# One wide product for a weight's high part, and h's transposes side by side, in a two-layer attention trunk

## The chip, the cores and the metric

The kernel runs on one core of one Trainium2 chip. Its time is the device time of one execution in microseconds, as the median of several runs. Next to it stands one profiled execution, in which every instruction of every engine has a start and a length.

The engines go by the profile's names. PE is TensorE's matmuls and PEld its weight loads (the stationary operand); DVE is VectorE, ACT is ScalarE, POOL is GpSimd and SP is SyncE, which here only issues DMAs. Each engine works through its own queue in order. TensorE writes only to PSUM, of which there are eight banks of 128 partitions by 512 float32 values.

## The reference

Two layers over 256 tokens of width 1024, batch 1. All is float32. In a layer:

```python
x = x + 0.5 * swiglu(rms_norm(x, ffn1_norm[l]), ffn1_w_gate[l], ffn1_w_up[l], ffn1_w_down[l])
h = rms_norm(x, mix_norm[l])
proj = h @ w_in[l]                       # 1024 -> 2304
qa, ka, va, qb, kb, vb = jnp.split(proj, SPLITS, axis=-1)
out_a = windowed_gqa_sink(qa, ka, va, sink[l], slopes_a)          # 8 query heads, 2 key/value heads
out_b = differential_attention(qb, kb, vb, lam, slopes_b)         # 4 heads, two softmaxes each
out_b = (rms_norm(out_b, diff_subln[l]) * (1.0 - lam_init)).reshape(b, s, B_V_COLS)
x = x + jnp.concatenate([out_a, out_b], axis=-1) @ w_out[l]
x = x + 0.5 * swiglu(rms_norm(x, ffn2_norm[l]), ffn2_w_gate[l], ffn2_w_up[l], ffn2_w_down[l])
```

A final `rms_norm` ends it. `swiglu` is `(silu(h @ w_gate) * (h @ w_up)) @ w_down` with an inner width of 2816.

## The kernel before

**Numbers in two parts.** A float32 operand is split into a high part, the value rounded to `float32r`, and a low part, the rest. ScalarE rounds (`act.copy`) and VectorE subtracts (`dve.tensor_tensor`). A product is then three matmuls: high by high, high by low and low by high. All weights come by DMA into `raw` tiles and are split so, piece by piece, in `emit_split`.

**FFN.** Each layer has two. The inner width goes in groups of 512. The gate and up products of most groups are done "by sevens" (`by_sevens`): seven block products over sums and differences of the four blocks of x and of the gate and up weights take the place of eight. The sums of weights are made partly by DMAs of GpSimd's queue that add while they write (`gather` in `seven`), partly by VectorE (`plus`). `sevens=(2, 3, 4)` in the first FFN and `(1, 2, 3, 4)` in the other three, so there are 15 such groups. In the three FFNs that begin with group 1 the first group (`start` in the code) has no earlier group to work off. In a group by sevens the order on TensorE is: `p1`, the first block product; transposes of the earlier group's hidden block `h`, one token half at a time (`turn_one`); down products of earlier groups (`below`), 24 matmuls each; and the other six block products (`prod`), 12 matmuls each. ScalarE writes −p1 into both banks of the PSUM tile `xy`, and later products add onto it there. What is transposed is copied out of PSUM as high part (ScalarE) and low part (VectorE).

**Attention.** `mix` runs the combined input projection in groups of 256 output columns: two of keys for the differential heads (`first_groups`), two of queries for them, one of keys and values and two of queries for the windowed heads (`ngroup`); these seven call `narrow`. A weight chunk of 128 by 128 is the stationary operand and x, transposed, the moving one, its high part in columns 0 to 255 and its low part in 256 to 511 of `xv`. Per chunk there are three matmuls of 256 columns that all add into the same half of a bank. The result is multiplied by the tokens' reciprocal norms `R` on VectorE and split (`rmul` and `k_finish` for keys, `q_finish` for queries). Then come the scores, softmax with the bias of distance, transposes of the weights, the products with the values, the norm of the differential heads and the output projection.

**The order.** TensorE's instructions keep the program's order throughout; the other engines keep it in the FFNs, and in the attention they are ordered by the tile framework's planner. Weight pieces are split ahead of their use by a table, `LEAD`: at each `go()` or `weights()` the kernel calls `ahead(n)`, which emits DMAs and splits up to half-step n. So the table sets where in the queues of ScalarE and VectorE the splits stand. `seven` lists the loads of one group in the order in which they are used.

**PSUM.** `bank()` takes one of six banks; `pair()` takes the remaining two as one tile of 128 by 2 by 512.

All instructions are recorded by one helper, line 62, so the profile shows that line for every one of them, and the tile names tell them apart: `w` are split weights, `s` blocks of 128 by 2 by 512 (x, h and others), `q` and `v` the summed blocks of x and the queries, `raw` loaded weights.

Of the kernel before, what the change touches and what calls it, by code (L numbers as in the profile page):

```python
# [14 lines left out]
P = 128  # L15
D = 1024
S = 256
# [11 lines left out]
N_RAW, N_S4 = 6, 28  # L29
IN_FFN, IN_MIX = 8, 6  # L30
SEVEN = ((2, 3, 4), (1, 2, 3, 4))
LEAD = dict(start=(2, 8, 11, 9),
            open0=(2, 2, 0, 2, 2, 4, 8, 6, 7, 7, 8, 9, 4, 4, 7, 7, 7, 0),
            first=(1, 6, 6, 9, 12, 16, 16, 19, 19, 20, 22),
            mid=(6, 9, 9, 12, 15, 15, 17, 20, 20, 23, 24),
            last=(1, 8, 9, 12, 15, 15, 16, 18, 20, 21, 21),
            mid0=(1, 8, 12, 14, 15, 15, 20, 20, 20, 22, 22),
            last0=(4, 8, 11, 12, 15, 15, 17, 18, 20, 24, 24),
            first0=(2, 3, 5, 5, 5, 12, 12, 12, 12, 13, 13),
            open=(5, 10, 7, 14, 9, 11, 9, 3),  # L40
            close0=(3, 7, 10, 10, 6, 10, 5, 9, 6, 8, 2, 7, 2),
            close=(0, 8, 9, 9, 7, 10, 6, 7, 7, 7, 3, 7, 5),
            mix=(9, 3, 0, 2, 9, 2, 3, 5, 6, 8, 5, 4, 6, 1, 6, 7, 0, 4, 1, 9, 7, 8, 6, 11, 9, 9))


@with_exitstack
def trunk(ctx: ExitStack, tc: tile.TileContext, x, n1, g1, u1, d1, nm, w_in, sink,
# [31 lines left out]
    def nm_(s):  # L79
        uid[0] += 1  # L80
        return f"{s}_{uid[0]}"
# [2 lines left out]
        return ps.tile([P, 512], F32, tag="ps", bufs=6, name=nm_("ps"))  # L84

    def pair():
        return ps.tile([P, 2, 512], F32, tag="xy", bufs=1, name=nm_("xy"))

    def halves(b):
        return b.rearrange("p (a n) -> p a n", a=2)  # L90
# [40 lines left out]
    def seven(wg, wu, c0, below, down):  # L131

        a, b, c, d = [object() for _ in range(4)]
        w = {a: rows(wg, c0, 512, 0, 4), b: rows(wu, c0, 512, 0, 4), c: rows(wu, c0, 512, 4, 4), d: rows(wg, c0, 512, 4, 4)}

        def load(k):
            return lambda t: [(t, w[k])]  # L140

        def gather(k, to):
            def add():
                pool.dma_start(raws[to], w[k], accum_op=ALU.add)
            return add

        def plus(x, to):
            def prep():
                dve.tensor_tensor(raws[to], raws[to], raws[x], op=ALU.add)
            return prep  # L150

        steps = [Step(4, 512, load(b), key=b, behind=gather(c, b)), down, Step(4, 512, load(d), key=d, free=[])]
        if below is not None:
            steps.insert(0, below)
        else:
            steps.insert(0, steps.pop())
        steps[0].prep = lambda: issue(gather(b, a), 1)
# [477 lines left out]
    def narrow(acc, w, j, xs, kcs, first, last):  # L635

        for i, (wk, xk) in enumerate(kcs):
            wh, wl = w.part(wk, h=j)
            xv = xs[xk // 2][:, xk % 2]
            pe.matmul(acc, lhsT=wh, rhs=xv[:, 0:S], start=first and i == 0 and j == 0, stop=False)  # L640
            pe.matmul(acc, lhsT=wh, rhs=xv[:, S:512], start=False, stop=False)
            pe.matmul(acc, lhsT=wl, rhs=xv[:, 0:S], start=False, stop=last and i == len(kcs) - 1 and j == 1)

    def first_groups(norm, ws):

        both = pair()
        sls = [halves(both[:, i]) for i in range(2)]
        for k in range(0, KC, 2):
            norm.late(k // 2)
            for w, sl in zip(ws, sls):  # L650
                for j in range(2):
                    narrow(sl[:, j], w, j, norm.xs, KALL[k:k + 2], k == 0, k == KC - 2)
        norm.spread(bank())
        return sls

    def ngroup(norm, w):
        sl = halves(bank())
        for j in range(2):
            narrow(sl[:, j], w, j, norm.xs, KALL, True, True)
        return sl  # L660

    class Residual:
# [24 lines left out]
    def ffn(norm, aside=None, before=None, final=False, sevens=SEVEN[1]):  # L687
# [31 lines left out]
                pe.matmul(acc, lhsT=xh, rhs=lo, start=False, stop=k == 3, skip_group_check=not first)  # L719
            return acc  # L720

        def turn_one(h, t):
            sl = bank()
            for k in range(4):
                pe.transpose(sl[:, k * P:(k + 1) * P], h[:, t, k * P:(k + 1) * P], ident)
            hb = blk()
            act.copy(hb[:, 0], sl)
            dve.tensor_tensor(hb[:, 1], sl, f(hb[:, 0]), op=ALU.subtract)
            return hb
# [14 lines left out]
        def by_sevens(h, groups, old):  # L744
# [5 lines left out]
            for g in groups:  # L750
                start, late = old is None, g == groups[-1]
                first = 2 * at["use"] - (2 if start else 0)
                caps = iter(LEAD[("first" if start else "last" if late else "mid") + "0" * (stage == 0)])

                def go():
                    ahead(first + next(caps))

                go()
                p1 = prod(norm.quarter(0, 0), take())
                act.activation(xy, p1.unsqueeze(1).to_broadcast([P, 2, 512]), AF.Copy, scale=-1.0)  # L760
                new = [turn_one(h, 0)]
                go()
                if start:
                    new.append(turn_one(h, 1))
                    go()
                    prod(norm.quarter(0, 1), take(), p1)
                else:
                    below(old, g - 2, 1, take())
                    new.append(turn_one(h, 1))
                    go()  # L770
                prod(norm.summed(0), take(), xy[:, 0])
                go()
                below(by_token(new), g - 1, 0, take())
                go()
                if not start:
                    prod(norm.quarter(0, 1), take(), p1)
                g0 = silu(flat(), p1, 0)
                go()
                old = by_token(new)
                p5 = prod(norm.summed(1), take())  # L780
                act.copy(p1, p5)
                go()
                prod(norm.summed(2), take(), xy[:, 1])
                go()
                prod(norm.summed(3), take(), p5)
                e = flat()
                act.copy(e, p5)
                u1, u0 = flat(), flat()
                dve.tensor_tensor(u0, xy[:, 1], e, op=ALU.add)
                dve.tensor_tensor(u1, xy[:, 0], e, op=ALU.add)  # L790
# [37 lines left out]
        def both():  # L828
            p = pair()
            return [p[:, t] for t in range(2)]  # L830

        gs, us = [bank(), bank()], both()
        if before is None:
            before = norm.late
        look[0] = IN_FFN
# [42 lines left out]
        for n in range(1, NGRP):  # L878
# [10 lines left out]
            tokens(gs, norm.xs, weights(), 4)  # L889
            g = gate(gs)  # L890
            next(sums, None)
            us = both()
            for k0 in (0, 4):
                tokens(us, norm.xs, weights(), k0)
                next(sums, None)
# [3 lines left out]
                if hh == 0:  # L899
                    next(sums, None)  # L900

        gu = both()
        tokens(gu, norm.xs, weights(), 0)
        hT = turn(h, 2)
        tokens(gu, norm.xs, weights(), 4)
# [53 lines left out]
    def mix(l, norm, nxt_norm):  # L959
# [7 lines left out]
            for i in range(n):  # L967
                kbs[names[i]] = kt[:, i]

        def rmul(sl):  # L970
            t = tmp()
            dve.tensor_tensor(t, sl, bc(norm.R), op=ALU.mult)
            return t

        def q_finish(sl, sc):
            t = tmp()
            q = tp.tile([P, 2, 512], F32R, tag="q", bufs=3, name=nm_("q"))
            with urgent():
                for i in range(2):
                    dve.scalar_tensor_tensor(t[:, i], in0=sl[:, i], scalar=sc[i], in1=norm.R, op0=ALU.mult, op1=ALU.mult)  # L980
                split(q, t)
            return [q[:, 0], q[:, 1]]

        def scores(q, kb, dist, slopes, init, den, wide=False):

            both = pair() if wide else None
            sl = [both[:, i] if wide else bank() for i in range(2)]
# [43 lines left out]

        s0, s1 = first_groups(norm, (weights(held=True), weights(2, True)))
        kept[0] = False
        k_finish(rmul(s0), 2, [("b", 0), ("b", 1)])
        k_finish(rmul(s1), 2, [("b", 2), ("b", 3)])
        q0 = q_finish(ngroup(norm, weights()), [qscB[:, 0:1], qscB[:, 1:2]])
        q1 = q_finish(ngroup(norm, weights()), [qscB[:, 2:3], qscB[:, 3:4]])
        tkv = rmul(ngroup(norm, weights()))
        a_b = [soft_b(0, q0[0]), soft_b(1, q0[1])]
        k_finish(tkv, 1, ["a"])  # L1040

# [29 lines left out]
        vsl = [both[:, t] for t in range(2)]  # L1071
        for k0 in (0, 4):
            w = weights()
            for k in range(4):
# [41 lines left out]

        oT = [blk() for _ in range(4)]
        rsl, both = [bank() for _ in range(2)], pair()
        osl = [both[:, t] for t in range(2)]
        for t in range(2):  # L1120
            for h in range(HB):
                for kc in range(2):
# [173 lines left out]
```

## Time and profile before

| | |
|---|---|
| median of 3 runs | 916.47 us (916.43 to 916.83) |
| the profiled execution | 916.47 us, of which the span is 914.7 us |
| TensorE busy | 906.1 us, 4710 matmuls |
| VectorE busy | 767.5 us |
| ScalarE busy | 600.1 us |
| DMA | 200.87 MB, mean 220 GB/s |

The page lists the busy time of each engine, then the chain of work that ended last, then groups of instructions: their count, their busy time, the mean length of one, and the idle time before them with what ended it. Matmuls are pipelined, so the mean length of a matmul (389 ns for 512 columns) is more than the distance from one start to the next; counting the distance needs the starts. In a timeline a row is the start in us, the time from the first start to the last end, the engine, and what it did, with the count.

### The profile page before, as it was taken

How to read it: one execution, taken by the hardware profiler on the slowest of the kernel's cores; microseconds unless marked ns; L12 is line 12 of the kernel's file. 1: busy time of each engine (PE TensorE's matmuls, PEld its weight loads, DVE VectorE, ACT ScalarE, POOL GpSimd, SP SyncE). 2: the span in 40 equal slices, each digit the busy share in tenths (PEclk: the TensorE clock that was granted, in tenths of full speed). 3: DMA queues.
4: the chain of work that ended last, by engine and by line, in shares of the span. 5: the costliest groups of instructions: out<-in, count | busy, mean ns of one | idle time of the engine just before them, and what ended most of it. 6: DMA issues, size and time to landing. Idle time of an engine off the chain costs nothing.

```text
span 914.7 us, 12449 instructions
## 1 busy us (share of the span) xinstructions
PE 906.1 (99%) x4710; PEld 766.4 (84%) x4710; DVE 767.5 (84%) x1033; ACT 600.1 (66%) x932; POOL 66.9 (7%) x83
## 2 busy tenths in 40 slices
PE   9999999999999999999999999999999999999997
PEld 8888888899888888888888888888998888888886
DVE  5959999778876899999688999996786878999984
ACT  6936778465875776677485676675576685776660
POOL 0501000000000101000010101000001010101011
PEclk9999999999999999999999999999999999999999
DMA  9998897953436798897858898897722758898821
GB/s 333 346 275 222 243 296 246 264 140 134 140 137 186 183 286 240 235 298 257 278 140 236 240 295 259 231 310 196 206 71 90 247 115 237 232 305 249 241 100 47
DMA packets 114061, 200.87 MB, mean 220 GB/s; under 512 B 3662, under 2 KB 31376, under 8 KB 114000
## 3 DMA queue, kind: packets, MB, share of 16 engines
q1 hardware_dynamic: 97344, 167.53, 54.0%
q0 software_dynamic: 16096, 31.75, 20.1%
q8 instruction: 37, 0.61, 0.3%
q10 hardware_dynamic: 560, 0.79, 0.2%
q14 instruction: 24, 0.20, 0.1%
HBM read 199.00 MB, written 1.05 MB: 219 GB/s over the span
## 4 chain that ended last, share of the span: by engine, by line
PE 98%; issue 0%; ACT 0%; DVE 0%; POOL 0%; POOLq 0%
PE ps L62 73%; PE xy L62 26%; ACT xy L62 0%; DVE s L62 0%; DVE xk L62 0%; POOLq L1291 0%; POOL rf L62 0%; POOL ident masks.py:199 0%; POOL ident masks.py:197 0%; DVE tot L62 0%; POOLq masks.py:199 0%; DVE tmp L62 0%; POOLq L1282 0%
## 5 line engine op out<-in xcount | busy, mean ns | idle before, releaser
L62 DVE TENSOR_TENSOR w<-raw,w 128x1024 fp32r<-128x1024 f32 (+1 forms) x458 | 478.9, 1098 | 39.5 <-ACT w L62 38.6
L62 PE MATMUL ps<-w,s 128*128 128x512 f32 (+1 forms) x2046 | 478.1, 390 | 0.7 <-ACT xy L62 0.7
L62 ACT CAST w<-raw 128x1024 fp32r<-128x1024 f32 (+1 forms) x458 | 404.5, 952 | 74.3 <-DVE raw L62 58.9
L62 PEld LDWEIGHTS ps<-w,s 128*128 128x128 f32 x2046 | 379.4, 188 | 78.9 <-ACT xy L62 1.4
L62 PE MATMUL xy<-w,s 128*128 128x512 f32 x528 | 125.8, 392 | 0.0
L62 PEld LDWEIGHTS xy<-w,s 128*128 128x128 f32 x528 | 98.3, 188 | 20.4
L62 PE MATMUL xy<-w,q 128*128 128x512 f32 x360 | 87.8, 393 | 0.0
L62 PEld LDWEIGHTS xy<-w,q 128*128 128x128 f32 x360 | 66.7, 188 | 13.4
L62 POOL DMA_DIRECT2D raw<-in_ffn_w_up_dram x30 | 38.9, 1314 | 422.5 <-DVE w L62 285.3
L62 DVE TENSOR_TENSOR raw<-raw,raw 128x2048 f32<-128x2048 f32 x30 | 68.6, 2288 | 0.5
L62 PE MATMUL ps<-s,w 128*128 128x256 f32 x480 | 59.2, 284 | 0.0
L62 PEld LDWEIGHTS ps<-s,w 128*128 128x128 f32 x480 | 58.1, 192 | 0.4
L62 ACT ACTIVATE s<-ps,gcol 128x256 fp32r<-128x256 f32 (+1 forms) x80 | 31.8, 478 | 40.2 <-PE ps L62 40.2
L62 ACT CAST s<-ps 128x512 fp32r<-128x512 f32 x44 | 24.9, 587 | 32.6 <-PE ps L62 32.6
L62 DVE TENSOR_TENSOR s<-ps,s 128x512 fp32r<-128x512 f32 x44 | 29.4, 684 | 18.7 <-ACT s L62 18.7
L62 PE MATMUL ps<-w,q 128*128 128x512 f32 x180 | 43.2, 389 | 0.0
L62 PE MATMUL ps<-w,v 128*128 128x512 f32 x180 | 43.2, 389 | 0.0
L62 PE MATMUL ps<-ident,s 128*128 128x128 f32 x304 | 41.2, 273 | 0.0
L62 PEld LDWEIGHTS ps<-ident,s 128*128 128x128 f32 x304 | 35.7, 141 | 6.1 <-issue 0.8
L62 PEld LDWEIGHTS ps<-w,q 128*128 128x128 f32 x180 | 33.8, 188 | 7.0
L62 PEld LDWEIGHTS ps<-w,v 128*128 128x128 f32 x180 | 33.8, 188 | 7.0
L62 ACT ACTIVATE s<-s,negm 128x256 f32<-128x256 f32 x64 | 31.8, 499 | 11.1 <-DVE negm L62 9.9
(120 smaller groups left out, 529.5 us busy)
## 6 DMA issues: line engine op xcount, KB each, us to landing
raw<-in_ffn_w_down_dram SPq DMA_DIRECT2D x44, 1024.0 KB, 6.6
raw<-in_ffn_w_gate_dram SPq DMA_DIRECT2D x39, 1024.0 KB, 6.8
raw<-in_ffn_w_up_dram SPq DMA_DIRECT2D x39, 1024.0 KB, 6.7
raw<-in_ffn_w_up_dram POOLq DMA_DIRECT2D x30, 1024.0 KB, 9.4
raw<-in_w_in_dram SPq DMA_DIRECT2D x14, 1024.0 KB, 5.6
raw<-in_ffn_w_gate_dram SPq DMA_DIRECT2D x8, 512.0 KB, 7.0
raw<-in_ffn_w_up_dram SPq DMA_DIRECT2D x8, 512.0 KB, 8.5
raw<-in_w_in_dram SPq DMA_DIRECT2D x8, 512.0 KB, 7.6
```

The source lines that it names most:

```text
L62: ins = issue(*a, **k)
```

## The change

Five things change.

1. In `narrow` the high part of a weight chunk is multiplied by both parts of x in one product of 512 columns, into a whole bank; the low part is multiplied by x's high part, 256 columns, and added to the bank's second half. A group of 256 output columns so fills two banks. The new `whole` adds the two halves of each bank: ScalarE copies the second half to SBUF, with the scale, VectorE adds the first half, and VectorE multiplies by `R`. `rmul` goes, and `q_finish` calls `whole`.
2. `pair()` becomes a list of two tiles of one bank each. Where ScalarE wrote −p1 to both banks by one instruction, two now write one bank each.
3. In a group by sevens that isn't the first, the transposes of both token halves stand together, after the down product; those of the second half go to `xy[1]`, which gets its −p1 later, after the product onto `xy[0]`. The transposes are issued as matmuls with `is_transpose`, with the start flag on the first of four and the stop flag on the last.
4. In a first group by sevens the product onto `xy[0]` is moved before the product that adds onto p1; in `seven` the two loads swap places.
5. Every row of the look-ahead table `LEAD` is rewritten.

```diff
 LEAD = dict(...
-            first=(1, 6, 6, 9, 12, 16, 16, 19, 19, 20, 22),
-            mid=(6, 9, 9, 12, 15, 15, 17, 20, 20, 23, 24),
+            first=(1, 1, 1, 7, 12, 15, 16, 19, 19, 22, 22),
+            mid=(2, 8, 12, 12, 15, 15, 20, 20, 20, 22, 23),
...
     def pair():
-        return ps.tile([P, 2, 512], F32, tag="xy", bufs=1, name=nm_("xy"))
+        return [ps.tile([P, 512], F32, tag="xy", bufs=2, name=nm_("xy")) for _ in range(2)]
...
         else:
-            steps.insert(0, steps.pop())
+            steps.insert(1, steps.pop())
...
             xv = xs[xk // 2][:, xk % 2]
-            pe.matmul(acc, lhsT=wh, rhs=xv[:, 0:S], start=first and i == 0 and j == 0, stop=False)
-            pe.matmul(acc, lhsT=wh, rhs=xv[:, S:512], start=False, stop=False)
-            pe.matmul(acc, lhsT=wl, rhs=xv[:, 0:S], start=False, stop=last and i == len(kcs) - 1 and j == 1)
+            pe.matmul(acc, lhsT=wh, rhs=xv, start=first and i == 0, stop=False)
+            pe.matmul(acc[:, S:512], lhsT=wl, rhs=xv[:, 0:S], start=False, stop=last and i == len(kcs) - 1)
...
-        both = pair()
-        sls = [halves(both[:, i]) for i in range(2)]
+        sls = [[bank(), bank()], pair()]
...
-                    narrow(sl[:, j], w, j, norm.xs, KALL[k:k + 2], k == 0, k == KC - 2)
+                    narrow(sl[j], w, j, norm.xs, KALL[k:k + 2], k == 0, k == KC - 2)
...
     def ngroup(norm, w):
-        sl = halves(bank())
+        sl = [bank(), bank()]
...
-        def turn_one(h, t):
-            sl = bank()
+        def turn_one(h, t, sl=None):
+            sl = bank() if sl is None else sl
             for k in range(4):
-                pe.transpose(sl[:, k * P:(k + 1) * P], h[:, t, k * P:(k + 1) * P], ident)
+                pe.matmul(sl[:, k * P:(k + 1) * P], lhsT=h[:, t, k * P:(k + 1) * P], rhs=ident,
+                          is_transpose=True, start=k == 0, stop=k == 3)
...
                 p1 = prod(norm.quarter(0, 0), take())
-                act.activation(xy, p1.unsqueeze(1).to_broadcast([P, 2, 512]), AF.Copy, scale=-1.0)
-                new = [turn_one(h, 0)]
+                act.activation(xy[0], p1, AF.Copy, scale=-1.0)
+                if start:
+                    act.activation(xy[1], p1, AF.Copy, scale=-1.0)
+                    new = [turn_one(h, 0)]
+                    go()
+                    new.append(turn_one(h, 1))
+                    go()
+                else:
+                    below(old, g - 2, 1, take())
+                    go()
+                    new = [turn_one(h, 0), turn_one(h, 1, xy[1])]
+                    go()
+                prod(norm.summed(0), take(), xy[0])
+                if not start:
+                    act.activation(xy[1], p1, AF.Copy, scale=-1.0)
                 go()
                 if start:
-                    new.append(turn_one(h, 1))
-                    go()
                     prod(norm.quarter(0, 1), take(), p1)
-                else:
-                    below(old, g - 2, 1, take())
-                    new.append(turn_one(h, 1))
-                    go()
-                prod(norm.summed(0), take(), xy[:, 0])
-                go()
                 below(by_token(new), g - 1, 0, take())
...
-        def rmul(sl):
+        def whole(sl, sc=(1.0, 1.0)):
+
             t = tmp()
-            dve.tensor_tensor(t, sl, bc(norm.R), op=ALU.mult)
+            for i, b in enumerate(sl):
+                act.activation(t[:, i], b[:, S:512], AF.Copy, scale=sc[i])
+            for i, b in enumerate(sl):
+                dve.scalar_tensor_tensor(t[:, i], in0=b[:, 0:S], scalar=sc[i], in1=t[:, i], op0=ALU.mult, op1=ALU.add)
+            dve.tensor_tensor(t, t, bc(norm.R), op=ALU.mult)
             return t

         def q_finish(sl, sc):
-            t = tmp()
             q = tp.tile([P, 2, 512], F32R, tag="q", bufs=3, name=nm_("q"))
             with urgent():
-                for i in range(2):
-                    dve.scalar_tensor_tensor(t[:, i], in0=sl[:, i], scalar=sc[i], in1=norm.R, op0=ALU.mult, op1=ALU.mult)
-                split(q, t)
+                split(q, whole(sl, sc))
             return [q[:, 0], q[:, 1]]
```

The remaining edits replace `xy[:, i]` and `both[:, t]` by the new pair's items.

More of the change, by code (lines that the diff above doesn't have):

```diff
@@ L31 @@
 SEVEN = ((2, 3, 4), (1, 2, 3, 4))
-LEAD = dict(start=(2, 8, 11, 9),
-            open0=(2, 2, 0, 2, 2, 4, 8, 6, 7, 7, 8, 9, 4, 4, 7, 7, 7, 0),
-            first=(1, 6, 6, 9, 12, 16, 16, 19, 19, 20, 22),
-            mid=(6, 9, 9, 12, 15, 15, 17, 20, 20, 23, 24),
[L36 to L43, printed above, removed]
+LEAD = dict(start=(5, 7, 10, 10),
+            open0=(2, 0, 0, 2, 6, 6, 8, 6, 5, 6, 1, 10, 2, 5, 7, 7, 8, 0),
+            first=(1, 1, 1, 7, 12, 15, 16, 19, 19, 22, 22),
+            mid=(2, 8, 12, 12, 15, 15, 20, 20, 20, 22, 23),
+            last=(1, 7, 12, 14, 15, 15, 17, 20, 20, 21, 22),
+            mid0=(6, 9, 12, 14, 15, 15, 19, 19, 19, 22, 24),
+            last0=(2, 8, 12, 13, 15, 15, 19, 20, 20, 23, 25),
+            first0=(2, 3, 3, 4, 7, 11, 11, 14, 14, 18, 18),
+            open=(8, 12, 11, 9, 11, 11, 9, 5),
+            close0=(7, 5, 7, 5, 6, 10, 3, 10, 5, 11, 4, 7, 1),
+            close=(1, 8, 9, 9, 6, 8, 8, 9, 1, 7, 5, 4, 6),
+            mix=(10, 2, 0, 2, 9, 2, 3, 5, 6, 11, 5, 2, 3, 1, 6, 5, 2, 4, 1, 6, 7, 8, 6, 11, 7, 8))
 @with_exitstack
@@ L656, in ngroup @@
     def ngroup(norm, w):
-        sl = halves(bank())
+        sl = [bank(), bank()]
         for j in range(2):
-            narrow(sl[:, j], w, j, norm.xs, KALL, True, True)
+            narrow(sl[j], w, j, norm.xs, KALL, True, True)
         return sl
@@ L782, in by_sevens @@
                 go()
-                prod(norm.summed(2), take(), xy[:, 1])
+                prod(norm.summed(2), take(), xy[1])
                 go()
@@ L788, in by_sevens @@
                 u1, u0 = flat(), flat()
-                dve.tensor_tensor(u0, xy[:, 1], e, op=ALU.add)
-                dve.tensor_tensor(u1, xy[:, 0], e, op=ALU.add)
+                dve.tensor_tensor(u0, xy[1], e, op=ALU.add)
+                dve.tensor_tensor(u1, xy[0], e, op=ALU.add)
                 h = blk(F32)
@@ L825, in down @@
             tokens(accs[h], [None] * (2 * g) + hT, w, 4 * g, last=(FC - 1, G4 - 1) if final and h else FC - 1)
[L828 to L832, printed above, removed]
+        gs, us = [bank(), bank()], pair()
         if before is None:
@@ L891, in ffn @@
             next(sums, None)
-            us = both()
+            us = pair()
             for k0 in (0, 4):
@@ L900, in ffn @@
                     next(sums, None)
-        gu = both()
+        gu = pair()
         tokens(gu, norm.xs, weights(), 0)
@@ L986, in scores @@
             both = pair() if wide else None
-            sl = [both[:, i] if wide else bank() for i in range(2)]
+            sl = [both[i] if wide else bank() for i in range(2)]
             for t in range(2):
@@ L1033, in mix @@
         kept[0] = False
-        k_finish(rmul(s0), 2, [("b", 0), ("b", 1)])
-        k_finish(rmul(s1), 2, [("b", 2), ("b", 3)])
+        k_finish(whole(s0), 2, [("b", 0), ("b", 1)])
+        k_finish(whole(s1), 2, [("b", 2), ("b", 3)])
         q0 = q_finish(ngroup(norm, weights()), [qscB[:, 0:1], qscB[:, 1:2]])
         q1 = q_finish(ngroup(norm, weights()), [qscB[:, 2:3], qscB[:, 3:4]])
-        tkv = rmul(ngroup(norm, weights()))
+        tkv = whole(ngroup(norm, weights()))
         a_b = [soft_b(0, q0[0]), soft_b(1, q0[1])]
@@ L1070, in mix @@
         both = pair()
-        vsl = [both[:, t] for t in range(2)]
+        vsl = both
         for k0 in (0, 4):
@@ L1118, in mix @@
         rsl, both = [bank() for _ in range(2)], pair()
-        osl = [both[:, t] for t in range(2)]
+        osl = both
         for t in range(2):
```

## The prediction

> **What bounds the kernel now.** I read the first part of the page, then the chain of work that ended last, then the waits.
>
> ```profile
> span 914.7 us, 12449 instructions
> PE 906.1 (99%) x4710; PEld 766.4 (84%) x4710; DVE 767.5 (84%) x1033; ACT 600.1 (66%) x932; POOL 66.9 (7%) x83
> PE 98%; issue 0%; ACT 0%; DVE 0%; POOL 0%; POOLq 0%
> ...
> PEld ps L62 <- ACT xy L62: 1.4, 3, 0.5
> ```
>
> TensorE works through the whole span and is 98% of the chain, so time leaves only as TensorE instructions, or as the small waits between them. VectorE has 16% of the span free and ScalarE 34%: room on average, not everywhere. The last row is a wait that the change touches: three times about 0.5 us before a weight load, on ScalarE's copy into `xy`.
>
> A busy TensorE may still run slowly, so the next thing is the spacing of matmuls, read off long unbroken pieces of the chain (start, length, count):
>
> ```profile
> 100.53 10.88 PE ps L62 x48
> ...
> 189.47 8.63 PE xy L62 x72
> ```
>
> 48 products of 512 columns take 10.88 us, 226.7 ns each; 72 of 256 columns take 8.63 us, 119.9 ns each. The difference, 106.8 ns for 256 columns, is 0.417 ns a column; what is left, 13.1 ns, comes with each instruction whatever its width.
>
> **Wide products.** The narrow ones are these two groups:
>
> ```profile
> L62 PE MATMUL ps<-s,w 128*128 128x256 f32 x480 | 59.2, 284 | 0.0
> L62 PE MATMUL xy<-s,w 128*128 128x256 f32 x192 | 23.8, 284 | 0.0
> ```
>
> 480 + 192 = 672 products are 224 triples (2 layers, 7 groups, 8 chunks, 2 halves). A triple becomes one product of 512 columns and one of 256: 3 × 119.9 = 359.7 ns against 226.7 + 119.9 = 346.6 ns. The columns stay, one instruction goes: 13.1 × 224 = 2.93 us, all on the path. A weight load goes with it; a load is hidden today behind every 119.9 ns product, so it is hidden behind a wider one.
>
> The Trainium skill, "TensorE: Matmul & The Clock Gate", section "Back-to-back issue gap", gives a warm matmul N/2.4 + 2.5 ns. By it the fixed part would be 2.5 ns, and the removed instructions an estimated 0.56 us; our rows disagree with its constant (13.1 ns), agree with its slope, and decide. By the page the sum below would be 914.3 us.
>
> **Transposes together.** In the groups by seven the two tokens' transposes stand apart today, with 24 products between; elsewhere eight stand together:
>
> ```profile
> 181.94 1.03 PE L62 MATMUL ps<-ident,xk 128*128 128x128 f32 x8
> 182.73 3.00 PE L62 MATMUL ps<-w,s 128*128 128x512 f32 x12
> 185.56 3.03 PE L62 MATMUL xy<-s,w 128*128 128x256 f32 x24
> ...
> 334.16 0.60 PE L62 MATMUL ps<-ident,s 128*128 128x128 f32 x4
> 334.51 5.74 PE L62 MATMUL ps<-w,s 128*128 128x512 f32 x24
> 340.09 0.60 PE L62 MATMUL ps<-ident,s 128*128 128x128 f32 x4
> 340.45 2.99 PE L62 MATMUL xy<-w,q 128*128 128x512 f32 x12
> 343.27 3.11 PE L62 MATMUL ps<-w,s 128*128 128x512 f32 x13
> ```
>
> From start to start, four cost 5.93 − 24 × 0.2267 = 0.49 us, and the next four 3.18 − 2.72 = 0.46: 0.95 together. Eight in one run cost 3.62 − 2.72 = 0.90. Leaving and entering transposes once less is worth 0.05 us. Of the 15 groups by seven three are first groups, where the eight already stand together, so 12 × 0.05 = 0.6 us. I cost the start and stop flags at nothing: the instruction and its shape stay.
>
> The price is that both halves of `h` are now finished in the 12 products before the down products, where one was. Today:
>
> ```profile
> 369.92 3.48 DVE L62 TENSOR_TENSOR w<-raw,w 128x1024 fp32r<-128x1024 f32 x3
> 373.33 0.68 DVE L62 TENSOR_TENSOR s<-ps,s 128x512 fp32r<-128x512 f32 x1
> ...
> 374.14 4.24 PE L62 MATMUL ps<-w,s 128*128 128x512 f32 x18
> ```
>
> The second half's subtraction ends at 374.01; the low part of that token is first wanted by the fifth product, 374.14 + 4 × 0.227 = 375.05. That is 1.0 us in hand; a further 128x512 subtraction in VectorE's queue takes 0.6 to 0.7. It fits with 0.3 to spare, if no more weight pieces (3.48/3 = 1.16 us each) stand ahead of it. I take nothing here, and price the other case as a rival. The second token's transposes go to `xy[1]`, so ScalarE's later write of −p1 there waits for that subtraction; behind it queue ScalarE's weight copies. ScalarE has a third of its time free, and p1 itself is first added to after another 24 products (5.4 us), so I take nothing there either.
>
> **The first groups.** Here the waits named above lie:
>
> ```profile
> 308.28 1.03 PE L62 MATMUL ps<-ident,s 128*128 128x128 f32 x8
> 309.54 3.02 PE L62 MATMUL ps<-w,s 128*128 128x512 f32 x12 [0.23 <-ACT xy L62]
> 312.39 2.88 PE L62 MATMUL xy<-w,q 128*128 128x512 f32 x12
> ...
> 308.48 1.01 ACT L62 ACTIVATE xy<-ps 128x1024 f32<-128x1024 f32 x1 [3.35 <-PE ps L62]
> ...
> L62 ACT COPY ps<-ps 128x512 f32<-128x512 f32 x15 | 8.6, 572 | 25.0 <-PE ps L62 25.0
> ```
>
> 4.11 − 2.72 = 1.39 us for eight transposes, 0.49 more than without a wait: the next product adds onto p1, which ScalarE reads until 309.49 to write both banks of `xy`. Reordered, the product onto `xy[0]` comes next. A PSUM copy of one bank takes 0.57 us, so `xy[0]` stands at 308.48 + 0.57 = 309.05; with the 0.05 us between ScalarE's end and TensorE's start now, TensorE resumes at 309.10, not 309.54. I take 0.44 × 3 = 1.3 us (at best 1.5; at worst 0, if the wait only changes its name). The second copy, 0.57 us, ends long before p1 is added to, 12 products later; it delays the two halves' copies on ScalarE by no more than today's double copy does. Late next are the weights of the step that is moved forward by 2.7 us, whose second part GpSimd's queue adds by DMA. That transfer is early:
>
> ```profile
> 276.34 1.34 POOL L62 DMA_DIRECT2D raw<-in_ffn_w_up_dram  x1 [17.91 <-DVE w L62]
> 297.91 1.32 POOL L62 DMA_DIRECT2D raw<-in_ffn_w_up_dram  x1
> raw<-in_ffn_w_up_dram POOLq DMA_DIRECT2D x30, 1024.0 KB, 9.4
> ```
>
> Issued at 276.34 and landing some 9.4 us later, it is over 20 us ahead of 309. SyncE's loads of the two steps swap places; no DMA is added.
>
> **Halves added by VectorE.** Each group of projections now has two ScalarE copies of 256 columns from PSUM, two VectorE operations and one multiplication, before the split.
>
> ```profile
> 182.00:260.00 78.00, 78.00 (x637) 71.99 (x636) 60.08 (x168) 50.04 (x137) 3.53 (x4) 1.00 0.42 122
> L62 ACT ACTIVATE s<-ps,gcol 128x256 fp32r<-128x256 f32 (+1 forms) x80 | 31.8, 478 | 40.2 <-PE ps L62 40.2
> L62 DVE SCALAR_TENSOR_TENSOR tmp<-ps,qscB,R 128x256 f32<-128x256 f32 x8 | 3.5, 476 | 0.0
> L62 DVE TENSOR_TENSOR tmp<-ps,R 128x512 f32<-128x512 f32 x2 | 1.4, 692 | 4.4 <-PE ps L62 4.4
> ...
> 215.84 0.69 DVE L62 TENSOR_TENSOR tmp<-ps,R 128x512 f32<-128x512 f32 x1 [2.20 <-PE ps L62]
> 239.48 0.48 DVE L62 CUSTOM_DVE_ANT_0 s<-ps,distA,nsnk 128x256 f32<-128x256 f32 x1
> 242.20 1.09 PE L62 MATMUL ps<-ident,s 128*128 128x128 f32 x8
> ```
>
> A layer's ScalarE gets 14 × 0.48 = 6.7 us more; VectorE 3 × (2 × 0.48) = 2.9 for key and value groups, whose multiplication stays (0.69), and 4 × 0.69 = 2.8 for the q groups, whose scaling moves into the additions: 5.7 us. In this layer the first row has VectorE busy for 60.08 of 78 us and ScalarE for 50.04: 18 and 28 us free. The early groups meet idle VectorE (2.20 us before 215.84 alone). The late ones do not: the last key-value group and both windowed q groups put 0.96 + 2 × 0.69 = 2.3 us into the softmax stretch. The nearest work behind it are the transposes at 242.20, whose banks come free when the second head pair's bias step ends, about 239.9: 2.3 us in hand, and TensorE comes 32 × 0.013 = 0.4 us earlier. So the need, 2.7, exceeds the margin by 0.4, less what VectorE's idle time in between and its movable weight pieces give back. Bounds: nothing, and 2.7 us a layer; I take 0.15, nearer nothing, 0.3 us in all. In PSUM a group holds two of six banks instead of one, free again some 2 us after its end while the group two later comes 5.5 us on: nothing.
>
> **The look-ahead table** is rewritten throughout. It adds and removes no work, only places weight pieces. Bounds: it can remove only the waits that remain, under 1 us; one piece put badly costs up to 1.2 us wherever a margin is short. I take zero, the first row having shown almost no wait to mend.
>
> **Sum.** −2.93 − 0.6 − 1.3 + 0.3 = −4.5 us. The profiled execution took 916.47 us around its 914.7 span, and the median of the runs is also 916.47: 912.0 us.
>
> **Rivals.** (1) Slower: the halves of `h` come late. If the new table leaves one more weight piece (1.16 us) ahead of the two subtractions, the 0.3 us to spare becomes a wait of 0.85 us in each of 12 groups, 10 us: 922 us. It decides from 0.5 us a group on (4.5 + 1.8 us over 12 reaches 918.3). For it: the queue above already holds three pieces in front. Against: today's order keeps 1.0 us in hand in every group, and VectorE's load there does not grow. 11%.
> (2) The projections' additions push the softmax: 0.7 to 2 us of wait a layer instead of 0.15, that is 913.1 to 915.7, about 914.3. For it: 2.7 against 2.3 above. Against: weight pieces fill that queue and can move. 14%.
> (3) The wide product saves nothing, the 13.1 ns being of switching operands and not of issue: 914.9 us. Against: both widths show the same remainder. By the skill's constant, 914.3, close to this case. 5%.
>
> **How the numbers follow.** The forecast, 910.9 to 913.4 (full waits gained and nothing lost; half the first groups' gain and 0.4 us more lost a layer), has 70%. A measurement tells 0.2%, 1.8 us, from no change: faster is below 914.6, slower above 918.3. Faster: 70 + 8 of (2) + 1 of (3) = 79%; slower: 10 of (1); same: the remaining 11%. The range, 910.6 to 916.0, adds (2) and (3) to the forecast and leaves out (1) and little else.
>
> **What would show it.** Products of 512 and 256 columns alternating at 346.6 ns a pair; 4486 matmuls, if all are recorded; TensorE's three waits on `xy` near 0.05 us; eight transposes at 0.90 us in 15 places; VectorE near 779 and ScalarE near 615 us. Wrong would be waits of the down products on VectorE's `s`, of scores or transposes on VectorE in the softmax stretch, or of any product on `w`.

## The result and the profile after

The changed kernel takes 911.84 us (median; 911.71 to 912.20) against 916.50 us, a ratio of 0.9949 with a 95% interval of 0.9932 to 0.9966: 4.66 us less. Timed again beside other kernels, it took 912.22 us against 916.50. The forecast was 912.0 us. Its profiled execution took 912.20 us, of which the span is 910.4 us.

The page and the weight loads' waits, in the order in which the prediction read them:

```profile
span 910.4 us, 12060 instructions
PE 902.3 (99%) x4486; PEld 754.2 (83%) x4486; DVE 777.5 (85%) x1053; ACT 613.8 (67%) x975; POOL 64.9 (7%) x83
...
PEld ps L62 <- issue: 3.3, 13, 0.4
PEld ps L62 <- POOL ident masks.py:199: 1.4, 1, 1.4
PEld ps L62 <- ACT tmp L62: 0.8, 2, 0.4
PEld ps L62 <- DVE s L62: 0.7, 1, 0.7
```

TensorE is still busy for the whole span, with 224 matmuls fewer. VectorE has 10.0 us more to do and ScalarE 13.7 us more, and the span is shorter all the same. The wait on ScalarE's `xy` is gone from the list. The largest new wait that names an engine came once: a weight load waited 0.7 us for VectorE's `s`. The row `issue` is time for which the profile names no cause.

The projections, where three groups follow one another and where one stands between scores. First the windows of the kernel before, then the same pieces after the change (first the stretch and its length, then each engine's busy time and count):

```profile
198.19:215.73 17.54, 17.54 (x146) 17.38 (x145) 13.88 (x24) 10.02 (x19) 0.00 (x0) 1.00 0.64 201
217.35:223.29 5.94, 5.94 (x50) 5.81 (x49) 5.02 (x23) 4.22 (x17) 0.00 (x0) 1.00 0.00 1
```

```profile
197.92:214.84 16.92, 16.92 (x98) 14.72 (x96) 16.57 (x30) 13.78 (x28) 0.00 (x0) 1.00 0.65 218
216.47:222.31 5.84, 5.84 (x34) 4.89 (x32) 5.77 (x26) 4.83 (x19) 0.00 (x0) 1.00 0.49 174
```

Three groups, 48 triples, became 0.62 us shorter, 12.9 ns a triple. The group between scores became only 0.10 us shorter, 6 ns for each of its 16 triples. Over an attention the start of the stage's transposes shows what is left at its end: 230.95 before, 229.87 after, and 185.56 and 185.66 for the first projection, so 1.18 us a layer, 2.3 to 2.4 in both.

The first group by seven that has no earlier group, after the change:

```profile
307.19 1.03 PE L62 MATMUL ps<-ident,s 128*128 128x128 f32 x8
308.02 3.01 PE L62 MATMUL xy<-w,q 128*128 128x512 f32 x12
310.87 1.30 PE L62 MATMUL ps<-w,s 128*128 128x512 f32 x5
...
307.39 1.07 ACT L62 ACTIVATE xy<-ps 128x512 f32<-128x512 f32 x2 [2.19 <-PE ps L62]
```

From the transposes to the end of the 12 products is 3.68 us, 0.96 without the products' 2.72, where it was 1.39. And a group that isn't the first, its transposes now eight in a row:

```profile
338.08 0.60 PE L62 MATMUL ps<-ident,s 128*128 128x128 f32 x4
338.51 0.60 PE L62 MATMUL xy<-ident,s 128*128 128x128 f32 x4
338.87 2.98 PE L62 MATMUL xy<-w,q 128*128 128x512 f32 x12
341.68 1.52 PE L62 MATMUL ps<-w,s 128*128 128x512 f32 x6
```

3.60 − 2.72 = 0.88 us, where two times four cost 0.95.

So the traces agree with each term to within 0.6 us: 2.3 to 2.4 us in the projections, 3 × 0.43 = 1.3 in the first groups, 12 × 0.05 to 0.07 in the others. What they can't show is what part of it the rewritten table carries.

### The profile page after: what moved, and what is told of

Same layout as the page of the kernel before. It is cut to its first block, busy times and chain, and to the rows that moved or that the text cites. A ratio compares the mean times of both kernels' runs of the same rounds, so it can differ in the third digit from the quotient of the medians.

```text
span 910.4 us, 12060 instructions
## 1 busy us (share of the span) xinstructions
PE 902.3 (99%) x4486; PEld 754.2 (83%) x4486; DVE 777.5 (85%) x1053; ACT 613.8 (67%) x975; POOL 64.9 (7%) x83
## 4 chain that ended last, share of the span: by engine, by line
PE 91%; DMA 5%; DVE 1%; ACT 1%; issue 1%; POOL 0%; SPq 0%; POOLq 0%; ACTq 0%
PE ps L62 69%; PE xy L62 22%; DMA raw<-in_ffn_w_up_dram 4%; DVE w L62 1%; DMA raw<-in_ffn_w_gate_dram 1%; ACT w L62 1%; ACT junk L62 0%; POOL r L62 0%; ACT s L62 0%; DVE s L62 0%; ACT tmp L62 0%; SPq L172 0%; DVE xk L62 0%; DVE q L62 0%; POOLq L1293 0%
## 5 line engine op out<-in xcount | busy, mean ns | idle before, releaser
L62 PE MATMUL ps<-s,w 128*128 128x512 f32 (+1 forms) x384 | 70.2, 339 | 0.0
L62 ACT CAST s<-ps 128x512 fp32r<-128x512 f32 x32 | 18.1, 593 | 36.5 <-PE ps L62 36.3
L62 DVE TENSOR_TENSOR s<-ps,s 128x512 fp32r<-128x512 f32 x32 | 21.3, 688 | 18.0 <-ACT s L62 17.9
L62 PE MATMUL ps<-ident,s 128*128 128x128 f32 x256 | 34.0, 273 | 0.0
L62 PEld LDWEIGHTS ps<-ident,s 128*128 128x128 f32 x256 | 29.7, 140 | 4.8 <-issue 0.8
```

The lines of the kernel that those rows point to most:

```text
L62: ins = issue(*a, **k)
```

## The experiments

The theory to test is the prediction's: the three edits save TensorE's time each by itself, and the table is worth nothing. The rivals are that the gain is the table's, or that the edits fit only together with it. Each kernel was timed in turn with the kernel before on the same chip; its ratio to that is given with its 95% interval.

**The wide product, issued as two.** From the changed kernel:

```diff
-            pe.matmul(acc, lhsT=wh, rhs=xv, start=first and i == 0, stop=False)
+            pe.matmul(acc[:, 0:S], lhsT=wh, rhs=xv[:, 0:S], start=first and i == 0, stop=False)
+            pe.matmul(acc[:, S:512], lhsT=wh, rhs=xv[:, S:512], start=False, stop=False)
```

> The changed kernel, with each wide product of 512 columns issued as two of 256; all else stays, the additions on VectorE and ScalarE too. Theory (each matmul instruction has a fixed part of 13.1 ns, on the path): 224 more instructions, 2.4 to 2.9 us slower than the changed kernel, 914.2 to 914.8 us. Rival (the gain came from the new table and the order, not from the instructions): no slower, 911.8 us.

914.25 us, 0.9978 (0.9969 to 0.9986) of before: 2.0 to 2.4 us more than the two medians of the changed kernel. Here the columns, the banks, the additions and the table are as in the changed kernel, so the 224 added products cost this. Each brings a weight load of its own (4710 of both again), and no run parts a product's price from its load's. The timeline has the three groups back at their old length:

```profile
197.55 17.61 PE L62 MATMUL ps<-s,w 128*128 128x256 f32 x144
215.09 0.98 PE L62 MATMUL ps<-s,q 64*128 64x256 f32 x12
```

215.09 − 197.55 = 17.54 us.

**The wide products alone.** The kernel before, with `narrow`, `whole`, the pair of two tiles and the two banks a group, and nothing else.

```diff
+            pe.matmul(acc, lhsT=wh, rhs=xv, start=first and i == 0, stop=False)
+            pe.matmul(acc[:, S:512], lhsT=wl, rhs=xv[:, 0:S], start=False, stop=last and i == len(kcs) - 1)
...
-        k_finish(rmul(s0), 2, [("b", 0), ("b", 1)])
+        k_finish(whole(s0), 2, [("b", 0), ("b", 1)])
```

> The kernel before with the wide products and the additions of halves alone; order, transposes and look-ahead table as before. Theory (the parts add up, and the table is worth nothing): 2.4 us faster than before, the amount by which the attention stages of the two traces differ, 914.1 us. Rival (the additions fit only with the new table): waits in the softmax stretch eat the gain, 915.5 us or more.

914.16 us, 0.9976 (0.9967 to 0.9985): 2.23 us less, with the interval some 1.4 to 3.0. The new work of VectorE and ScalarE costs no time that shows, with the old table too.

**The first groups alone.**

```diff
-            steps.insert(0, steps.pop())
+            steps.insert(1, steps.pop())
...
-                act.activation(xy, p1.unsqueeze(1).to_broadcast([P, 2, 512]), AF.Copy, scale=-1.0)
+                act.activation(xy[0], p1, AF.Copy, scale=-1.0)
+                act.activation(xy[1], p1, AF.Copy, scale=-1.0)
...
+                prod(norm.summed(0), take(), xy[0])
+                go()
                 if start:
                     prod(norm.quarter(0, 1), take(), p1)
-                prod(norm.summed(0), take(), xy[:, 0])
-                go()
```

> The kernel before with the new order in the three first groups by sevens alone, the split pair that it needs, and the old table. Theory (the wait for p1's copy goes, and nothing takes its place): 3 times 0.43 us less, 915.2 us. Rival (with the old table the weights of the step that moves forward are late): 916.5 us or more, with a wait on w.

914.84 us, 0.9984 (0.9975 to 0.9993): 1.55 us less. The weights that are now wanted earlier are there with the old table: its list of waits has no new row on `w`.

**The transposes alone, with the old table and with four rows of the new one.** Both kernels change `turn_one` and the order in groups that aren't the first:

```diff
-                new = [turn_one(h, 0)]
+                    below(old, g - 2, 1, take())
                     go()
-                    below(old, g - 2, 1, take())
-                    new.append(turn_one(h, 1))
+                    new = [turn_one(h, 0), turn_one(h, 1, xy[1])]
                     go()
```

The second also has the rows `mid`, `last`, `mid0` and `last0` of the new table, which rule these groups.

> The kernel before with the transposes of both halves of h together alone; narrow products, the order of the first groups and the table as before. Theory (0.05 us less in each of 12 groups, and with the old table 1.1 us of wait in the third group of three FFNs, as in the changed kernel with the old table): 916.4 - 0.6 + 3.3 = 919.1 us, with TensorE waiting for VectorE's s. Rival (that wait came from the table's other rows or from the wide products): 915.8 us and no such wait.

> The same with the four rows of the new table that rule the groups by seven which are not first. Theory (the rows put the weight pieces behind the halves of h): no wait on s, 916.4 - 0.6 = 915.8 us. Rival (the rows serve something else): as without them, 919 us.

With the old table 919.32 us, 1.0032 (1.0020 to 1.0045): 2.87 us slower. With the four rows 916.11 us, 0.9997 (0.9988 to 1.0006): 0.34 us less than before by the medians, which the interval can't tell from nothing. In the timeline of the first, TensorE stands in the third group of an FFN, and the waits name VectorE:

```profile
371.64 2.99 PE L62 MATMUL xy<-w,q 128*128 128x512 f32 x12
374.46 0.39 PE L62 MATMUL ps<-w,s 128*128 128x512 f32 x1
375.45 2.78 PE L62 MATMUL ps<-w,s 128*128 128x512 f32 x11 [0.60 <-DVE s L62]
...
PEld ps L62 <- DVE s L62: 3.4, 5, 1.0
```

The third groups of three FFNs have about 1.0 us each of the 3.4 us; the other two waits are short. With the four rows no wait on `s` is left in the list. So this edit loses time without the table, and at best gains little with it.

**The changed kernel with the old table.** `LEAD` as before the change, all else as after.

> The changed kernel with the old look-ahead table. Theory (the table is worth nothing by itself): within 0.5 us of the changed kernel, 911.4 to 912.3 us. Rival (the table bought the margin for the halves of h): waits of the down products on VectorE's s in the groups by sevens, 0.2 us or more in each of 12, 914 us or more.

915.49 us, 0.9991 (0.9983 to 1.0): 3.3 to 3.7 us slower than with the new table, so the theory that the table is worth nothing fell here. VectorE's queue around the third group, and TensorE's, with the old table and then with the new one:

```profile
367.27 0.74 DVE L62 SCALAR_TENSOR_TENSOR s<-tmp,hr,tmp 128x512 f32<-128x512 f32 x1
367.94 4.62 DVE L62 TENSOR_TENSOR w<-raw,w 128x1024 fp32r<-128x1024 f32 x4
372.48 0.68 DVE L62 TENSOR_TENSOR s<-ps,s 128x512 fp32r<-128x512 f32 x1
373.08 0.68 DVE L62 TENSOR_TENSOR s<-xy,s 128x512 fp32r<-128x512 f32 x1
...
368.63 0.60 PE L62 MATMUL ps<-ident,s 128*128 128x128 f32 x4
372.25 0.39 PE L62 MATMUL ps<-w,s 128*128 128x512 f32 x1
373.21 3.03 PE L62 MATMUL ps<-w,s 128*128 128x512 f32 x12 [0.57 <-DVE s L62]
```

```profile
364.95 0.75 DVE L62 SCALAR_TENSOR_TENSOR s<-tmp,hr,tmp 128x512 f32<-128x512 f32 x1
365.61 4.62 DVE L62 TENSOR_TENSOR w<-raw,w 128x1024 fp32r<-128x1024 f32 x4
370.15 0.68 DVE L62 TENSOR_TENSOR s<-ps,s 128x512 fp32r<-128x512 f32 x1
370.75 0.68 DVE L62 TENSOR_TENSOR s<-xy,s 128x512 fp32r<-128x512 f32 x1
```

With either table four weight pieces stand between the row that writes the second part of `h` (`s<-tmp`) and the two subtractions. What differs is when VectorE gets there. The first subtraction starts 3.85 us after the first transpose with the old table (372.48 − 368.63) and 1.26 us after it with the new one (370.15 against 368.89 in that trace). Its result is first wanted by the second down product, which stands 3.85 us after the first transpose when nothing waits; with the old table it is finished 0.7 us too late, with the new one 1.9 us ahead.

The lag of 2.6 us has two parts. The smaller is one weight piece, 1.2 us: the old table puts three of them ahead of that last write of `h`, the new one two. The larger part is a wait in the second group, the one before. ScalarE's and VectorE's rows there, right behind the transposes, again first with the old table and then with the new:

```profile
341.53 0.58 ACT L62 ACTIVATE xy<-ps 128x512 f32<-128x512 f32 x1 [2.01 <-DVE s L62]
342.03 3.89 ACT L62 CAST w<-raw 128x1024 fp32r<-128x1024 f32 x4
343.10 3.50 DVE L62 TENSOR_TENSOR w<-raw,w 128x1024 fp32r<-128x1024 f32 x3 [1.60 <-ACT w L62]
```

```profile
339.69 3.90 ACT L62 CAST w<-raw 128x1024 fp32r<-128x1024 f32 x4
343.48 0.59 ACT L62 ACTIVATE xy<-ps 128x512 f32<-128x512 f32 x1
340.77 4.63 DVE L62 TENSOR_TENSOR w<-raw,w 128x1024 fp32r<-128x1024 f32 x4 [0.15 <-ACT w L62]
```

With the old table ScalarE's write of −p1 to `xy[1]` stands ahead of its weight copies. It waits 2.01 us for VectorE's subtraction, and VectorE then waits 1.60 us for the first of those copies. The new table puts four copies ahead of the write, and VectorE waits 0.15 us. The three FFNs that begin with group 1 are alike in this. In the rows `mid` of the diff above this is the second and third number: 9 and 9 before, so nothing is emitted between the transposes and the write, and 8 and 12 after. The 1.45 us between the two waits and the 1.2 us of the piece make up the lag. No run changes one of the two alone; by these rows either by itself would still have left the first subtraction in time (1.26 + 1.2 or 1.26 + 1.45, and 0.68 for itself, are under 3.85).

**The table's other rows.** The kernel before with the rows `start`, `open0`, `open`, `close0`, `close` and `mix` of the new table.

> The kernel before with six rows of the new table, for the FFNs' beginnings and ends and for the attention; the rows for the groups by seven stay. Theory (only the first stage gains, 0.3 us, as the first transposes of the changed kernel come 0.28 us earlier): 916.1 us. Rival (these rows carry a part of the gain): 915.6 us or less.

916.31 us, 0.9998 (0.9989 to 1.0007): no difference that can be told, in the kernel before. The four rows took 3.2 us off the kernel with the transposes alone (919.32 to 916.11), and the whole table 3.3 to 3.7 off the changed one, so the four carry most of what the table is worth there. The row `first` was not tried alone; the row `first0` is used by no group.

**More work ahead of the halves of h.** The changed kernel with needless additions on VectorE, four or three in each of the 12 groups:

```diff
+                    for _ in range(4):
+                        dve.tensor_tensor(tmp("junk", 1, (P, 512)), xk[:, 0, 0:512], xk[:, 1, 0:512], op=ALU.add)
                     new = [turn_one(h, 0), turn_one(h, 1, xy[1])]
```

> The changed kernel with four needless additions of 512 elements (2.6 us) on VectorE ahead of the two subtractions, in the 12 groups by sevens that are not first. Theory (the halves of h have 1.9 us in hand in nine of these groups and 0.1 to 1.7 in the first FFN's three, and a wait begins where that ends): 9 x 0.7 + 3 x 1.6 = 11 us slower, 923 us. Rival (VectorE's queue has room that gives the delay back, or the down products don't depend on it): under 914 us.

> As with four needless additions ahead of the halves of h, but three (2.15 us a group). Theory (VectorE is 29.5 of 30.8 us busy in a group by sevens, 1.3 us are free, and what exceeds that is carried from group to group): (3 x 2.15 - 3 x 1.3) x 4 = 10 us slower, 922 us. Rival (each group alone decides, with 1.9 us in hand): 5 us slower, 917 us.

934.07 us, 1.0193 (1.0179 to 1.0207), with four, and 923.72 us, 1.0080 (1.0066 to 1.0094), with three. With four it came out at twice what was expected, and that made the second theory, which was then tested with three: 922 expected, 923.7 measured, and 917 by the rival. In this theory VectorE's whole group decides, and not the one place ahead of the down products. The reason stands in the windows of two groups in a row of the changed kernel, and of the one with four additions:

```profile
338.08:368.89 30.81, 30.81 (x141) 25.60 (x140) 29.50 (x28) 21.85 (x26) 2.57 (x2) 1.00 0.90 259
368.89:399.72 30.83, 30.83 (x142) 25.61 (x141) 29.53 (x28) 21.02 (x25) 2.57 (x2) 1.00 0.90 264
```

```profile
345.04:376.92 31.88, 31.11 (x142) 25.53 (x141) 30.62 (x31) 21.35 (x26) 2.57 (x2) 1.00 0.90 247
376.92:410.31 33.39, 31.16 (x142) 25.53 (x141) 32.14 (x32) 21.24 (x26) 2.57 (x2) 1.00 0.90 252
```

The third engine figure is VectorE: 29.5 of 30.8 us. A group has 1.3 us free on it. What is added beyond that isn't caught for long by the 1.9 us in hand at one place; it is carried into the next group, and the group itself becomes longer. The same sum for four additions, 2.87 us in their row, is (3 × 2.87 − 3 × 1.3) × 4 = 18.8 us, where 22 were measured. Most of the rest is in its trace: after two of the waits 35 products took 9.88 and 9.75 us in place of 8.27, at a lower granted clock, 3.1 us together (the last section has one of them).

**More work in the softmax stretch.** The changed kernel, with six multiplications by one after the last three groups' additions:

```diff
             dve.tensor_tensor(t, t, bc(norm.R), op=ALU.mult)
+            for _ in range(extra[0]):
+                dve.tensor_scalar_mul(t, t, 1.0)
             return t
```

> The changed kernel with six needless multiplications by one (512 elements, some 0.42 us each) on VectorE after the additions of each of a layer's last three projection groups: 7.6 us more a layer in the softmax stretch. Theory (in the changed kernel the second head pair's bias step ends 3.2 us ahead of the transposes that need its banks, and VectorE idles for about 3 us between scores and those transposes): some 1.5 to 4.5 us of wait a layer, 915 to 921 us. Rival (the projections' work on VectorE and the softmax aren't tied): 911.8 us.

920.85 us, 1.0045 (1.0032 to 1.0059): inside what the theory allowed, and the tie is real. But the place was another than expected. TensorE waited for the key-value group's own result, at its transposes, and for a windowed q, at its scores, not at the transposes behind the softmax:

```profile
225.02 0.44 PE L62 MATMUL ps<-ident,tmp 128*128 128x128 f32 x2 [1.64 <-DVE tmp L62]
...
236.12 1.58 PE L62 MATMUL ps<-s,q 64*128 64x256 f32 x22 [1.08 <-DVE q L62]
```

**The products sorted.** The changed kernel with the eight wide products of a half group first and the eight narrow ones after them:

```diff
+        for low in range(2):
             for i, (wk, xk) in enumerate(kcs):
...
+                if low:
+                    pe.matmul(acc[:, S:512], lhsT=wl, rhs=xv[:, 0:S], start=False, stop=last and i == len(kcs) - 1)
+                else:
+                    pe.matmul(acc, lhsT=wh, rhs=xv, start=first and i == 0, stop=False)
```

> The changed kernel with a half group's products sorted: all wide ones first, then all narrow ones. Theory (a wide product's weights must be loaded within a narrow product's 120 ns, and where that slips, in the two groups after scores, a pair takes 353 ns and not 346.7): those groups become 0.1 us shorter each, 911.4 us. Rival (the slower pairs come from something beside the alternation, as the softmax's traffic): no change, 911.8 us, the wide products there still above 230 ns.

912.16 us, 0.9951 (0.9939 to 0.9964): no gain that can be told. In its trace the group between scores takes 22.36 − 16.58 = 5.78 us instead of 5.84:

```profile
216.58 5.85 PE L62 MATMUL ps<-s,w 128*128 128x512 f32 x32
222.36 0.98 PE L62 MATMUL ps<-s,q 64*128 64x256 f32 x12
```

A group of 16 triples should have become 16 × 13.1 ns = 0.21 us shorter and became 0.10 shorter; sorting gives back 0.06 of the 0.11 that are missing, and 0.05 to 0.06 in each of the four groups after scores. But the stretch of three groups, which had no such loss, takes 17.04 us here and not 16.92. So the alternation has a part in the slower pairs, sorting costs elsewhere what it gives there, and the rest of the loss stays open.

**The changed kernel again.**

> The changed kernel as it is. Theory (the 0.5 us of wait of the first FFN's first down product in its profile follows a late DMA of that one execution): 911.8 us and no such wait in this profile. Rival (the table leaves it there): the wait again.

912.22 us, 0.9953 (0.9941 to 0.9966), and no wait on `s` in its profile. Two things differ there. ScalarE's weight copies had waited 10.04 us for a DMA in the first profile of the changed kernel, here 9.70; and TensorE comes to that group's transposes 0.49 us later (66.04 against 65.55), so it needs the result later. Which of the two took the wait away is open.

## Why the prediction was right

The time came out within 0.2 us, and the terms that made it are those measured. Beside them, two things that were set to nothing were worth about 3 us each, and cancel; there the sum was right by luck. One figure doesn't follow from the words beside it: all waits gained and nothing lost is 916.47 − 2.93 − 0.6 − 1.5 = 911.4 us, not 910.9. The measured time lies above both.

*Wide products*: 2.93 us forecast. Alone they gave 2.23 us, taken away again 2.0 to 2.4, and the traces 2.3 to 2.4. The mechanism, a fixed part for each product with its weight load, is shown by the kernel that issues the product as two. The size was 0.5 us too large, because the 13.1 ns were taken for all triples; in the two groups after scores, and in the first eight triples of a layer, only about half is saved. The Trainium skill, "TensorE: Matmul & The Clock Gate", section "Back-to-back issue gap", has 2.5 ns for the fixed part of a matmul measured by itself, an estimated 0.56 us for 224 instructions; 2.0 to 2.4 us were measured, and the measurement decides.

*First groups*: 1.3 us forecast, 3 × 0.43 in the traces and 1.55 by the run alone. About 0.06 us of the wait is left (0.96 − 0.90), as worked out: ScalarE's copy of one bank still ends a little after the transposes.

*Transposes together*: 0.6 us forecast, 0.34 by the run with the four rows, of which the interval allows nothing too; the trace has 0.05 to 0.07 a group. The step that failed is the one on ScalarE's write of −p1 to `xy[1]`, which "waits for that subtraction; behind it queue ScalarE's weight copies", and for which the prediction took "nothing there either". With the old table this held up the copies, and VectorE lost 1.60 us to them in the second group, where it has 1.3 us free in all. With the old table's pieces ahead of them, the halves' low parts then came late in the third group. That group became about 1.2 us longer in three FFNs, and the edit by itself cost 2.87 us. The step "It fits with 0.3 to spare" held in the second group, where no product waited. So the halves of `h` did come late, as in rival (1), but with the old table and not the new, in three groups and not in twelve, and with ScalarE's write as the step that the prediction had at nothing. That this write tips the third group over is read from rows; no run changes it alone.

*The look-ahead table*: "I take zero" was wrong as well: in the changed kernel it is worth 3.3 to 3.7 us, most of it in the four rows of these groups. It removes no wait of the kernel before, which is what was looked at; it removes the one that the moved transposes would have made. This is the luck in the sum: with the transposes moved and the table kept, the time was 915.5 us and not 911.8.

*Softmax stretch*: 0.3 us forecast as loss, none measured, with the old table or the new. Rival (2) could have been: 7.6 us more work a layer cost some 4.4 us a layer. But the margin was read at the wrong instruction: what fell due first were the transposes of the key-value group, and then the scores of a windowed group.

Rival (3), that the instruction isn't what costs, is refuted by the product issued as two. The sum of the parts run alone, 2.23 + 1.55 + 0.34 + 0.19 for the other rows, is 4.3 us; the whole gave 4.3 to 4.7. Each part has an interval of about 0.8 us to either side, so the agreement is closer than the runs can show.

## What to carry to other kernels

When TensorE is busy throughout, count instructions as well as columns: here each matmul, with its weight load, carried some 13 ns beside its columns in long runs, and taking one away gave 9 to 11 ns over all. The additions that fewer of them needed fitted on engines with room in that stage. Read the room of an engine from the stage and not from the whole span: VectorE was 85% busy over all and 96% in the groups by seven, and there a delay is carried on instead of absorbed. And when a step is moved, look at what is queued ahead of its results after the move, and at every instruction that now waits for them: what stands behind such an instruction in its engine's queue waits too, and the delay can come back to the engine that it began on (here 2.01 us on ScalarE became 1.60 us on VectorE). A table that sets that order has to be rewritten with it, and its worth can't be read from the waits of the kernel before.

## What was not expected of the hardware

After some idle times of 2.2 to 2.3 us, TensorE ran at a lower granted clock for some microseconds. In the kernel with four additions, one of 2.26 us was followed by this (the clock is the third figure from the right of each row):

```profile
102.21 0.39 PE L62 MATMUL ps<-w,s 128*128 128x512 f32 x1
104.86 6.47 PE L62 MATMUL ps<-w,s 128*128 128x512 f32 x20 [2.26 <-DVE s L62]
...
100.00:104.80 4.80, 2.60 (x12) 1.80 (x10) 4.70 (x8) 3.14 (x4) 0.00 (x0) 1.00 1.05 393
104.80:109.90 5.10, 5.04 (x15) 4.00 (x16) 5.10 (x6) 1.53 (x2) 1.28 (x1) 0.67 0.26 53
109.90:115.00 5.10, 5.10 (x24) 4.19 (x23) 5.01 (x5) 2.23 (x3) 0.00 (x0) 1.00 1.07 196
```

The clock is 0.67 in that stretch, and 0.50 from 106.86 to 108.86 us. The same trace has four idle times of 2.20 to 2.26 us; two were followed by a lower clock (at 105 and 564 us) and two were not (at 383 and 840 us). What decides is open. The Trainium skill, "TensorE: Matmul & The Clock Gate", section "What's actually happening", has the clock halve after an idle window of about 3.4 us that runs free of the kernel. The lowering to 0.50 agrees, but 2.26 us of idle time sufficed here.

At the kernel's beginning the same first six products took from 5.79 to 7.46 us in one profile of the changed kernel and to 7.98 in another. So the first stage alone moves by 0.5 us from one execution to the next, and the 0.28 us by which the first transposes came earlier in the first profile say nothing of the table.
